# Where side steps stand between matmuls: other rates for two lanes, and three longer waits in steps

## The chip, the cores and the metric

The kernel runs on one core of a Trainium2 chip. The metric is the device time of one execution in microseconds (us). Runs of this kernel are compared by their medians. The engines are called as the profile calls them: PE is the matrix engine (PEld its weight loads), DVE the vector engine, ACT the scalar engine, POOL the general engine, and SP the engine that here issues nearly all DMAs, in the order in which they stand in its queue.

## The reference, cut to what matters

One layer of a hybrid encoder works on two request groups, which share their weights: `x_sample` (1024 rows) and `x_prompt` (256 rows), each of width 2048.

```
hn   = rms_norm(x);  proj = hn @ w_in
xbc, z_ssd, dt_raw, q, k, v, z_att, mq, z_mem = split_cols(proj)
y    = ssd_scan(forward) + ssd_scan(backward) + d_skip * xs      # chunks of 128, 16 heads, running sums of dt * A
o_ssd = rms_norm(y * silu(z_ssd))
o_att = window_attention(norm(q), norm(k), v, sink) * silu(z_att) # |t - s| <= 128, 8 heads, 2 key heads
mk, mv = split_cols(rms_norm(mem) @ w_mem_kv)
o_mem = softmax(norm(mq) @ norm(mk)^T) @ mv * silu(z_mem)         # 4 heads, 256 memory rows
out   = x + concat[o_ssd, o_att, o_mem] @ w_out
```

Everything is float32. A product with a weight matrix is made of three reduced-precision products, from a high and a low part of each factor.

## The kernel before

**Tiles and blocks.** The 1280 rows are 10 tiles of 128: tiles 0 to 7 are `x_sample`, 8 and 9 `x_prompt`. The big products run over groups of five tiles, group 0 (tiles 0 to 4) and group 1 (tiles 5 to 9). The program is a row of blocks: the memory keys and values, part of group 0 in `block_pair` units (a seven-product scheme), the blocks `kv` and `z1` of group 0, then group 1 (`x0` to `x5`, `kv`, `q`, `za`, `z0`, `z1`, `mq`, `zm`), then the output blocks `o` and the output in pairs. A block loops over 16 slices `k` of the width. For each slice SP loads a weight tile `wraw` (four buffers), ACT makes its high part `wh` (L206), DVE the low part `wl` (L207, three buffers each), and PE makes the products (L258 to L260, or L293 to L295) into PSUM tiles `acc`.

**Lanes.** All other work (key preparation, attention, memory attention, the scan) is cut into steps by `yield` and stands in two queues, the lanes. Lane 0 holds `vectors`, `distances`, `mk_prep`, `k_prep`, `attn`, `mem_attn`; lane 1 holds `dt_prep`, `ssd_up`, `ssd_down`. After each slice `pump` runs steps: the table `RATES` gives, for each group and block, how many steps of lane 0 and of lane 1 a slice pays for (half as many per slice in the blocks that `feat` runs, which are `x`, `za` and `zm`).

```
owed[i] = owed[i] + rates[i] if lanes[i] else 0.0
while max(owed) >= 1: ...
    step(lanes[i])
```

So a `yield` is a place where products of the block are put between what a step has issued and what the next step issues. A bare `yield` more makes the distance longer by one step of that lane, and puts every later step of the lane back by one. `need(fn, ts)` runs the lanes until the named work is done, whatever the rates say. The instructions then go through a scheduler that may move them a little within their engine's order; the order on an engine is fixed when the kernel is built.

**The three places of the change.** `mk_prep` (L428) prepares one 128-row tile of the memory keys: SP loads it (`mkr` from `mr`, L430), ACT squares it (L436), DVE sums (L437), POOL takes a power (L123, L124), DVE scales twice (L442, L443), and after two bare yields PE turns the four heads (`pmk`, L448). `dt_prep` (L518) computes the steps `dt` of five tiles in a long chain of small DVE operations, has POOL make a triangular mask, and after one bare yield PE forms the running sums (`pacs`, L557 to L559). `ssd_down` (L1012) first issues the loads for one tile of the backward scan, among them the turned diagonal product (`ydT` from `yd`, L1035), and after three bare yields (five for the first tile of a request, `last`) `norm_ssd` scales the tile before, and `diag_in` has PE turn the loaded tile (`pd`, L1041), which DVE adds.

Of the kernel before, what the change touches and what calls it, by code (L numbers as in the profile page):

```python
# [28 lines left out]
CH, WB, RB, WA, WBB = 4, 3, 4, 5, 4  # L29
RBB = 4  # L30

RATES = ({'kv': (2.0, 1.0), 'z1': (3.0, 1.6)},
         {'kv': (1.4, 1.5), 'x': (2.1, 2.15), 'q': (2.2, 2.5), 'za': (2.05, 2.5), 'z0': (2.0, 2.6),
          'z1': (1.9, 2.65), 'mq': (1.9, 2.8), 'zm': (1.9, 2.85), 'o': (1.95, 2.1)})
FAR = 1e30

UNITS = (0, 8, 1, 9, 2, 10, 3, 11, 4, 12, 5, 13, 6, 7)
# [7 lines left out]
def hymba_encoder_kernel(  # L45
# [37 lines left out]
    def psum(name):  # L83
        return mix.tile([P, 512], F32, tag="mix", name=name)
# [37 lines left out]
    def rsqrt(dst, src, scale, n):  # L122
        G.tensor_scalar(out=dst, in0=src, scalar1=scale, scalar2=EPS, op0=ALU.mult, op1=ALU.add)  # L123
        G.tensor_tensor(out=dst, in0=dst, in1=mhalf[:, :n], op=ALU.pow)  # L124

    def hv(ap, n=8):
        return ap.rearrange("p (h d) -> p h d", h=n)

    def hb(ap, n, d):
        return ap.unsqueeze(2).broadcast_to([P, n, d])  # L130
# [90 lines left out]
    def w_in_rows(name):  # L221
        return w_laid(laid_in(name), W_AT[name][1])
# [107 lines left out]
    def ev_dtkv(base):  # L330
        def f(i, ps):
            t = base + i
            r = ev.tile([P, P], F32, tag="evt" if i % 2 else "evu", name="kraw")
            A.activation(r, ps[:, 32:160], AF.Copy)
            S.dma_start(k_d[t], r)
            V.tensor_add(dt_all[:, t, :], ps[:, :32], dtb)
            V.tensor_copy(v_all[:, i + (2 if base else 0), :], ps[:, 160:288])
        return f
# [76 lines left out]
    def w2(name):  # L415
        return mp.tile([P, 512], F32, tag="wa", name=name, bufs=WA)
# [11 lines left out]
    def mk_prep(i):  # L428
        kr = w2("mkr")
        S.dma_start(kr, mr_d[i])  # L430
        yield
        yield
        ss = sm.tile([P, 4], F32, tag="s4", name="ss", bufs=4)
        sq = w2("sq")
        rm = rx[:, 10 + i:11 + i]
        A.activation(sq, kr, AF.Square, scale=rm)  # L436
        V.reduce_sum(out=ss, in_=hv(sq, 4), axis=AX.X)  # L437
        r = sm.tile([P, 4], F32, tag="s4", name="r", bufs=4)
        rsqrt(r, ss, 1.0 / P, 4)
        yield  # L440
        yield
        V.scalar_tensor_tensor(out=hv(kr, 4), in0=hv(kr, 4), scalar=rm, in1=hb(r, 4, P), op0=ALU.mult, op1=ALU.mult)  # L442
        V.tensor_mul(hv(kr, 4), hv(kr, 4), gm.unsqueeze(1).broadcast_to([P, 4, P]))  # L443
        yield
        yield
        ps = psum("pmk")
        for h in range(4):
            T.transpose(ps[:, h * P:(h + 1) * P], kr[:, h * P:(h + 1) * P], ident)  # L448
        c = slice((i % 2) * P, (i % 2) * P + P)
        if i < 2:  # L450
            A.activation(mkH[:, :, c], hv(ps, 4), AF.Copy)
            V.tensor_sub(mkL[:, :, c], hv(ps, 4), mkH[:, :, c].bitcast(F32))
        else:
            o = w2("mko")
            A.activation(o, ps, AF.Copy)
            S.dma_start(mk_d[:, :, c], hv(o, 4))
        yield
# [60 lines left out]
    def dt_prep(t0):  # L518
        grp = t0 // 5
        ts = slice(t0, t0 + 5)  # L520
        flat = lambda a: a[:, ts, :].rearrange("p t h -> p (t h)")
        t6 = (t0 + 1) % 6
        wj, dd = [a[:, t6:t6 + 5, :].rearrange("p t h -> p (t h)") for a in (wj_all, dd_all)]
        t5 = lambda a: a.rearrange("p (t h) -> p t h", t=5)
        x = flat(dt_all)
        e, s = [mp.tile([P, 512], F32, tag="xs", name=n, bufs=2)[:, :160] for n in "es"]
        w, l = [mp.tile([P, 512], F32, tag="ya", name=n, bufs=2)[:, :160] for n in "wl"]
        V.scalar_tensor_tensor(out=e, in0=x, scalar=-1.0, in1=x, op0=ALU.mult, op1=ALU.min)
        A.activation(e, e, AF.Exp)
        V.tensor_scalar(out=s, in0=e, scalar1=2.0, scalar2=None, op0=ALU.add)  # L530
        V.reciprocal(out=s, in_=s)
        V.tensor_mul(s, s, e)
        V.tensor_mul(w, s, s)
        V.tensor_scalar(out=e, in0=w, scalar1=1.0 / 17, scalar2=None, op0=ALU.mult)
        for c in (15, 13, 11, 9, 7, 5, 3):
            V.scalar_tensor_tensor(out=e, in0=e, scalar=1.0 / c, in1=w, op0=ALU.add, op1=ALU.mult)
        V.scalar_tensor_tensor(out=e, in0=e, scalar=1.0, in1=s, op0=ALU.add, op1=ALU.mult)
        V.tensor_scalar(out=e, in0=e, scalar1=2.0, scalar2=None, op0=ALU.mult)
        V.scalar_tensor_tensor(out=x, in0=x, scalar=0.0, in1=e, op0=ALU.max, op1=ALU.add)
        yield  # L540

        da = e
        V.tensor_mul(t5(da), dt_all[:, ts, :], aneg.unsqueeze(1).broadcast_to([P, 5, 32]))
        yield

        V.tensor_scalar(out=w, in0=x, scalar1=1e-30, scalar2=None, op0=ALU.max)
        V.tensor_scalar(out=l, in0=w.bitcast(I32), scalar1=math.log(2.0) / 2 ** 23, scalar2=-126.957 * math.log(2.0),
                        op0=ALU.mult, op1=ALU.add)
        yield
        yield  # L550
        lower = w2("lower")[:, :P]
        G.affine_select(out=lower, in_=ones, compare_op=ALU.is_ge, fill=0.0, base=0,
                        pattern=[[-1, P]], channel_multiplier=1)
        yield
        ps = psum("pacs")
        p5 = t5(ps[:, :160])
        T.matmul(p5[:, :, 0:16], upper, t5(da)[:, :, 0:16], start=True, stop=True)  # L557
        T.matmul(p5[:, :, 16:32], lower, t5(da)[:, :, 16:32], start=True, stop=True)
        T.matmul(ps[:, 160:320], ones, da, start=True, stop=True)  # L559
        ac = wb("ac", shape=(P, 512))  # L560
        A.activation(ac[:, :320], ps[:, :320], AF.Copy)
        for _ in range(2):
            A.activation(s, l, AF.Exp)
            d = da
            V.tensor_sub(d, w, s)
            V.tensor_add(s, w, s)
            V.reciprocal(out=s, in_=s)
            V.tensor_mul(d, d, s)
            V.scalar_tensor_tensor(out=l, in0=d, scalar=2.0, in1=l, op0=ALU.mult, op1=ALU.add)
        A.activation(flat(eacs_all), ac[:, 0:160], AF.Exp)  # L570
        A.activation(flat(cd_all), ac[:, 160:320], AF.Exp)
        V.tensor_sub(wj, l, ac[:, 0:160])
        V.tensor_add(dd, wj, ac[:, 160:320])
        A.activation(dd, dd, AF.Exp)
        yield
        ps = psum("pact")
        T.transpose(ps[:, :P], ac[:, 0:128], ident)
        T.transpose(ps[:32, P:2 * P], ac[:, 128:160], ident)
        acT = wb("acT", shape=(P, 512))
        A.activation(acT[:, :P], ps[:, :P], AF.Copy)  # L580
        A.activation(acT[:32, P:2 * P], ps[:32, P:2 * P], AF.Copy)
        S.dma_start(ac_d[grp][0:P, :], acT[:, :P])
        S.dma_start(ac_d[grp][P:160, :], acT[:32, P:2 * P])
        yield
# [216 lines left out]
    def wb(name, dtype=F32, shape=(P, 512)):  # L801
        return mp.tile(list(shape), dtype, tag="wb", name=name, bufs=WBB)
# [207 lines left out]
    def ssd_down(t):  # L1010
        first = t in (0, NS)
        last = t in (NS - 1, NT - 1)  # L1012
# [28 lines left out]
                T.transpose(ps[:, j * P:(j + 1) * P].bitcast(F32R), ld[g][3][:, j, :], identr)  # L1041
            V.tensor_add(ld[g][0], ld[g][0], ps)

        for _ in range(5 if last else 3):
            yield
        norm_ssd()
        diag_in(0)
# [1 line left out]
        for g in range(2):  # L1049
            c = slice(g * 512, (g + 1) * 512)  # L1050
            y, z, st, _ = ld[g]
# [461 lines left out]
    def tok(name, w, evac, after=None, grp=0):  # L1513
        run(block_tok(w, 5, evac), RATES[grp][name], after)

    def feat(name, b, evac, grp, after=None, extra=None):
        run(block_feat(f"{name}{b}", evac), [r / 2 for r in RATES[grp][name]], after, lag=3, extra=extra)

# [7 lines left out]
    for u, unit in enumerate(units):  # L1526
# [42 lines left out]
    w_kv = w_in_rows("kv")  # L1569
    run(block_tok(w_kv, 5, ev_dtkv(0), before_last=lambda _: need(vectors, [0])), RATES[0]["kv"], hold=5,  # L1570
        extra=lambda k: some_left() if left else None)
# [4 lines left out]
    def when_done(n, then):  # L1576
# [11 lines left out]
    queue(0, mem_attn, range(5))  # L1588
    run(block_tok(w_in_rows("z1"), 5, ev_gate(1, 0)), RATES[0]["z1"], refill_x(1),
        extra=when_done(1, lambda: queue(1, ssd_up, range(4))))  # L1590
# [12 lines left out]
    kv_shift()  # L1603
    run(block_tok(w_kv, 5, ev_dtkv(5)), RATES[1]["kv"], extra=lambda k: some_left() if left else None)
    queue(0, k_prep, range(5, 10))
    queue(0, attn, [4])
    queue(1, dt_prep, [5])
    run(block_tok(w_in_rows("q"), 5, ev_raw(q_d, 5)), RATES[1]["q"], extra=when_done(2, lambda: queue(1, ssd_up, range(4, 8))))
    gate("za", 0)
# [108 lines left out]
```

## Time and profile before

| | |
|---|---|
| median of 3 runs | 1802.68 us (1802.52 to 1804.86) |
| the profiled execution's own time | 1801.42 us |
| span of the profile | 1799.7 us |
| PE busy | 1779.4 us, 10838 matmuls |
| DVE, ACT, POOL busy | 1249.6, 920.7, 545.1 us |
| granted PE clock | 1.0 |
| moved by DMA | 301.12 MB, mean 167 GB/s |

PE is busy in all but about 20 us of the span, so the time is what PE has to do, and what it waits for. The list of waits names each wait by who ended it, with the total, the number of times and the longest; windows give busy times by stage; the timeline shows single instructions. Where an engine's wait ended on something that the profile cannot name, it says "issue". Matmuls overlap, so the times of single ones add up to more than the time that PE is busy; from start to start is what one costs.

### The profile page before, as it was taken

To read this page: it belongs to the slowest core of one execution; us is meant where nothing else is said; L and a number is where in the kernel's file an instruction comes from. 1 tells how busy PE (TensorE), PEld (TensorE's weight loads), DVE (VectorE), ACT (ScalarE), POOL (GpSimd) and SP (SyncE) were. 2 spreads that over 40 slices of the span, in tenths; PEclk is the share of its full clock that TensorE was granted. 3 is DMA by queue.
4 is the path that set the end of the run, shared out by engine and by line. 5 is a ranking of instruction groups with operands and counts; after the bars stand their busy time and mean duration, and the time that the engine had idled before them with its cause. 6 is when DMAs were issued, how large, how long until landed. Compare 5 with 4: busy or idle time off the path is not lost.

```text
span 1799.7 us, 31431 instructions
## 1 busy us (share of the span) xinstructions
PE 1779.4 (99%) x10838; PEld 1605.1 (89%) x10838; DVE 1249.6 (69%) x2358; ACT 920.7 (51%) x2049; POOL 545.1 (30%) x900
## 2 busy tenths in 40 slices
PE   9999999999999999999999999999999999999999
PEld 7789999999997989999889977777878888889999
DVE  5595788888758887877675566567774644766665
ACT  6554455555325765757464466534374533443332
POOL 0105789989710210000000000001100000058775
PEclk9999999999999999999999999999999999999999
DMA  8653455444446645444645545558685765644442
GB/s 296 192 179 120 139 152 151 136 150 152 125 146 201 193 136 167 121 141 121 183 143 163 177 152 168 192 162 256 218 253 169 235 186 151 205 149 147 143 145 77
DMA packets 208207, 301.12 MB, mean 167 GB/s; under 512 B 19568, under 2 KB 86192, under 8 KB 208048
## 3 DMA queue, kind: packets, MB, share of 16 engines
q1 hardware_dynamic: 207904, 299.06, 53.9%
q8 instruction: 85, 1.39, 0.3%
q14 instruction: 74, 0.61, 0.1%
q10 hardware_dynamic: 144, 0.06, 0.0%
HBM read 236.36 MB, written 62.69 MB: 166 GB/s over the span
## 4 chain that ended last, share of the span: by engine, by line
PE 82%; issue 5%; DMA 5%; DVE 4%; ACT 3%; POOL 1%; SPq 0%; ACTq 0%; DVEq 0%; POOLq 0%
PE acc L258 9%; PE acc L259 9%; PE acc L260 9%; PE acc L1231 7%; PE acc L1233 7%; PE acc L1232 7%; PE acc L293 4%; PE acc L295 4%; PE acc L294 4%; PE accm L1232 3%; PE accm L1231 3%; PE accm L1233 3%; PE po L671 1%; PE pmo L780 1%; PE ppt L661 1%
## 5 line engine op out<-in xcount | busy, mean ns | idle before, releaser
L207 DVE TENSOR_TENSOR wl<-wraw,wh 128x512 fp32r<-128x512 f32 (+1 forms) x480 | 346.0, 723 | 236.4 <-ACT wh L206 223.5
L206 ACT ACTIVATE wh<-wraw 128x512 fp32r<-128x512 f32 (+1 forms) x480 | 292.2, 614 | 311.1 <-PE acc L260 155.9
L258 PE MATMUL acc<-wh,xH 128*128 128x512 f32 (+1 forms) x1088 | 418.7, 385 | 0.0
L259 PE MATMUL acc<-wl,xH 128*128 128x512 f32 (+1 forms) x1088 | 413.0, 380 | 0.9 <-DVE wl L207 0.8
L260 PE MATMUL acc<-wh,xL 128*128 128x512 f32 (+1 forms) x1088 | 409.9, 377 | 0.0
L259 PEld LDWEIGHTS acc<-wl,xH 128*128 128x128 f32 x1088 | 204.8, 188 | 40.5 <-issue 3.6
L260 PEld LDWEIGHTS acc<-wh,xL 128*128 128x128 f32 x1088 | 204.3, 188 | 38.1 <-issue 1.7
L258 PEld LDWEIGHTS acc<-wh,xH 128*128 128x128 f32 x1088 | 204.6, 188 | 37.4 <-issue 3.3
L293 PE MATMUL acc<-xH,wh 128*128 128x320 f32 x640 | 201.7, 315 | 0.0
L206 ACT ACTIVATE sh<-ws 128x384 fp32r<-128x384 f32 x176 | 91.3, 523 | 212.5 <-POOL ws L1203 107.5
L294 PE MATMUL acc<-xL,wh 128*128 128x320 f32 x640 | 199.2, 311 | 0.0
L295 PE MATMUL acc<-xH,wl 128*128 128x320 f32 x640 | 198.6, 310 | 0.0
L207 DVE TENSOR_TENSOR sl<-ws,sh 128x384 fp32r<-128x384 f32 x176 | 124.2, 709 | 100.7 <-ACT sh L206 96.7
L1203 POOL TENSOR_TENSOR ws<-wraw 128x128 f32<-128x128 f32 x176 | 109.4, 622 | 213.2 <-DMA wraw<-in_w_in_pairs_dram 87.1
L633 POOL COPY lg<-nsink 128x2 f32<-128x2 f32 x40 | 17.1, 428 | 386.9 <-PE ppt L661 139.4
L293 PEld LDWEIGHTS acc<-xH,wh 128*128 128x128 f32 x640 | 120.2, 188 | 2.6 <-issue 2.0
L294 PEld LDWEIGHTS acc<-xL,wh 128*128 128x128 f32 x640 | 120.3, 188 | 1.5 <-issue 1.2
L295 PEld LDWEIGHTS acc<-xH,wl 128*128 128x128 f32 x640 | 120.2, 188 | 1.2 <-issue 1.1
L1203 POOL TENSOR_TENSOR ws<-wraw,ws 128x128 f32<-128x128 f32 x176 | 116.6, 663 | 13.8
L1203 POOL TENSOR_TENSOR ws<-ws,wraw 128x128 f32<-128x128 f32 x176 | 116.1, 660 | 0.0
L1203 POOL TENSOR_TENSOR wraw<-wraw 128x128 f32<-128x128 f32 x176 | 111.2, 632 | 13.7
L362 DVE SCALAR_TENSOR_TENSOR c<-u,vec,c 128x638 f32<-128x638 f32 (+1 forms) x96 | 89.6, 936 | 15.2 <-ACT c L357 14.9
(437 smaller groups left out, 3941.9 us busy)
## 6 DMA issues: line engine op xcount, KB each, us to landing
wraw<-in_w_in_laid_dram SPq DMA_DIRECT2D x176, 256.0 KB, 3.0
wraw<-in_w_in_pairs_dram SPq DMA_DIRECT2D x112, 256.0 KB, 2.8
wraw<-in_w_out_laid_dram SPq DMA_DIRECT2D x64, 256.0 KB, 3.0
wraw<-in_w_out_pairs_dram SPq DMA_DIRECT2D x64, 256.0 KB, 2.7
rf<-ac SPq DMA_DIRECT2D x40, 256.0 KB, 3.8
rb<-ac SPq DMA_DIRECT2D x40, 256.0 KB, 4.9
wraw<-in_w_mem_laid_dram SPq DMA_DIRECT2D x32, 256.0 KB, 4.6
xst<-in_x_sample_dram SPq DMA_DIRECT2D x20, 256.0 KB, 5.0
```

What stands on the lines that cost most here:

```text
L206: a = A.activation(h, raw, AF.Copy)
L207: b = V.tensor_sub(l, raw, h.bitcast(F32))
L258: T.matmul(ps[t][:, :n], sh, h[:, :n], start=(k_ == 0), stop=False)
L259: T.matmul(ps[t][:, :n], sh, l[:, :n], start=False, stop=False)
L260: T.matmul(ps[t][:, :n], sl, h[:, :n], start=False, stop=(k_ == KT - 1))
L293: T.matmul(o, sh, cur["H", q][:, m, c], start=(k == 0), stop=False)
L294: T.matmul(o, sh, cur["L", q][:, m, c], start=False, stop=False)
L295: T.matmul(o, sl, cur["H", q][:, m, c], start=False, stop=(k == KT - 1))
L1203: G.tensor_tensor(out=o, in0=x, in1=y, op=op)
L1231: T.matmul(ps[p], h, xh, start=(k_ == 0), stop=False)
L1232: T.matmul(ps[p], h, xl, start=False, stop=False)
L1233: T.matmul(ps[p], l, xh, start=False, stop=(k_ == 7))
```

## The change

The table of rates gets other numbers for four blocks, and three places get further bare yields. In group 0's `kv` block lane 0 goes from 2.0 to 4.0 steps a slice; in `z1` after it from 3.0 to 2.2, and lane 1 from 1.6 to 1.7. In group 1, lane 0 goes from 1.9 to 1.6 in `zm`; in the output blocks `o` from 1.95 to 2.15 and lane 1 from 2.1 to 2.25. `mk_prep` waits three steps instead of two before its transposes, `dt_prep` two instead of one before its running sums, and `ssd_down` nine instead of five before its first diagonal product, in the first tile of a request only. No instruction is added to or taken from the computation.

```
-RATES = ({'kv': (2.0, 1.0), 'z1': (3.0, 1.6)},
+RATES = ({'kv': (4.0, 1.0), 'z1': (2.2, 1.7)},
          {'kv': (1.4, 1.5), 'x': (2.1, 2.15), 'q': (2.2, 2.5), 'za': (2.05, 2.5), 'z0': (2.0, 2.6),
-          'z1': (1.9, 2.65), 'mq': (1.9, 2.8), 'zm': (1.9, 2.85), 'o': (1.95, 2.1)})
+          'z1': (1.9, 2.65), 'mq': (1.9, 2.8), 'zm': (1.6, 2.85), 'o': (2.15, 2.25)})
...
         V.tensor_mul(hv(kr, 4), hv(kr, 4), gm.unsqueeze(1).broadcast_to([P, 4, P]))
+        yield
         yield
         yield
         ps = psum("pmk")
...
                         pattern=[[-1, P]], channel_multiplier=1)
+        yield
         yield
         ps = psum("pacs")
...
-        for _ in range(5 if last else 3):
+        for _ in range(9 if last else 3):
             yield
         norm_ssd()
         diag_in(0)
```

In the orders below, line numbers of the changed kernel are higher by one behind the first new line and by two behind the second.

**SP, around the load of the fourth tile of memory keys (`mr_198`), in group 0's `z1` block.** `wraw` is a weight tile, `rf` and `rb` are rows of running sums spread over all partitions, `chd` a slice of the turned input. Before:

```order
L213 DMA wraw<-in_w_in_laid_dram 128x512
L848 DMA rf<-ac_193 128x512
L188 DMA chd<-in_x_turned_dram 128x640 x2
L848 DMA rb<-ac_193 128x512
L213 DMA wraw<-in_w_in_laid_dram 128x512
L848 DMA rf<-ac_193 128x512
L848 DMA rb<-ac_193 128x512
L213 DMA wraw<-in_w_in_laid_dram 128x512
L848 DMA rb<-ac_193 128x512 x2
L430 DMA mkr<-mr_198 128x512
```

And in the changed kernel:

```order
L335 DMA k_146<-kraw 128x128
L335 DMA k_147<-kraw 128x128
L335 DMA k_148<-kraw 128x128
L213 DMA wraw<-in_w_in_laid_dram 128x512 x3
L430 DMA mkr<-mr_198 128x512
L457 DMA mk_d<-mko 512x1x128
L213 DMA wraw<-in_w_in_laid_dram 128x512 x2
L188 DMA chd<-in_x_turned_dram 128x640
```

The load has moved from behind the spread rows and the input slices to ahead of them; the PE order puts the transposes that need it 90 products behind the start of `z1`, where they stood at 157.

**DVE, at the end of group 0's `kv` block.** `wl` of 128x288 is the low part of one of this block's 16 weight tiles, the first of 128x512 belongs to `z1`; `ss`, `mkr` and `mkL` are `mk_prep`'s, `dist` and `pdist` are `distances`'. Before, the last four tiles of the block:

```order
L207 TENSOR_TENSOR wl<-wraw,wh 128x288 x2
L1462 CAST dist<-disti 128x384
L1463 SCALAR_TENSOR_TENSOR dist<-dist 128x384
L207 TENSOR_TENSOR wl<-wraw,wh 128x288 x2
L1470 CAST pdist<-dist 128x384
L207 TENSOR_TENSOR wl<-wraw,wh 128x512
L437 TENSOR_REDUCE ss<-sq 128x4
L336 TENSOR_TENSOR dt_all<-acc,dtb 128x32
```

In the changed kernel, the last three:

```order
L207 TENSOR_TENSOR wl<-wraw,wh 128x288
L437 TENSOR_REDUCE ss<-sq 128x4
L442 SCALAR_TENSOR_TENSOR mkr<-mkr,rx,r 128x512
L207 TENSOR_TENSOR wl<-wraw,wh 128x288
L443 TENSOR_TENSOR mkr<-mkr,state 128x512
L207 TENSOR_TENSOR wl<-wraw,wh 128x288
L437 TENSOR_REDUCE ss<-sq 128x4
L453 TENSOR_TENSOR mkL<-pmk,mkH 128x4x128
L442 SCALAR_TENSOR_TENSOR mkr<-mkr,rx,r 128x512
L443 TENSOR_TENSOR mkr<-mkr,state 128x512
L207 TENSOR_TENSOR wl<-wraw,wh 128x512
L336 TENSOR_TENSOR dt_all<-acc,dtb 128x32
```

The DVE work of three tiles of memory keys now stands between the weight tiles of `kv`, ahead of the evacuation of the block's results (L336).

**SP, at the loads for tile 4 of the backward scan, at the end of group 1's `mq` block.** `yd_176` is that tile's diagonal product in DRAM, `so` a finished output tile on its way out, `zd` a gate, `st` a state. Before:

```order
L1033 DMA st_14576<-sb_186 128x512
L1033 DMA st_14584<-sb_186 128x512
L275 DMA wraw<-in_w_in_laid_dram 128x512
L1029 DMA zd<-z_4_112 128x512
L1008 DMA oT_1_161<-so 512x1x128
L698 DMA oT_1_155<-oT 512x1x128
L1035 DMA ydT<-yd_176 128x512
```

And in the changed kernel:

```order
L1028 DMA zd<-yT 128x4x128
L1019 DMA cc<-xbc_d 128x2x128
L1035 DMA st_14642<-sb_186 128x512
L1010 DMA oT_1_161<-so 512x1x128
L1037 DMA ydT<-yd_176 128x512
L1025 DMA yd<-yp_166 128x512
L1035 DMA st_14650<-sb_186 128x512
L1031 DMA zd<-z_4_112 128x512
```

The load of the diagonal product now stands ahead of the gate's load instead of behind it; on PE its use has moved from 187 to 210 products behind the start of `mq`.

More of the change, by code (lines that the diff above doesn't have):

```diff
@@ L30 @@
 RBB = 4
-RATES = ({'kv': (2.0, 1.0), 'z1': (3.0, 1.6)},
+RATES = ({'kv': (4.0, 1.0), 'z1': (2.2, 1.7)},
          {'kv': (1.4, 1.5), 'x': (2.1, 2.15), 'q': (2.2, 2.5), 'za': (2.05, 2.5), 'z0': (2.0, 2.6),
-          'z1': (1.9, 2.65), 'mq': (1.9, 2.8), 'zm': (1.9, 2.85), 'o': (1.95, 2.1)})
+          'z1': (1.9, 2.65), 'mq': (1.9, 2.8), 'zm': (1.6, 2.85), 'o': (2.15, 2.25)})
 FAR = 1e30
@@ L445, in mk_prep @@
         yield
+        yield
         ps = psum("pmk")
@@ L553, in dt_prep @@
                         pattern=[[-1, P]], channel_multiplier=1)
+        yield
         yield
@@ L1042, in diag_in @@
             V.tensor_add(ld[g][0], ld[g][0], ps)
-        for _ in range(5 if last else 3):
+        for _ in range(9 if last else 3):
             yield
```

## The prediction

> **What bounds the kernel now.** I read the page first, then the busy times by stage, then PE's list of waits, then the timeline around the longest of them. The page gives each engine's busy time, and of the chain that ended last the shares:
>
> ```profile
> PE 1779.4 (99%) x10838; PEld 1605.1 (89%) x10838; DVE 1249.6 (69%) x2358; ACT 920.7 (51%) x2049; POOL 545.1 (30%) x900
> PE 82%; issue 5%; DMA 5%; DVE 4%; ACT 3%; POOL 1%; SPq 0%; ACTq 0%; DVEq 0%; POOLq 0%
> ```
>
> PE is the bound. The change adds no instruction to it, so it can only act on the time in which PE stands. Busy times by stage (columns: stretch and length, PE, PEld, DVE, ACT, POOL with counts, clock, DMA share, GB/s) show where that is; the rows are group 0's `kv`, its `z1`, and `x` of group 1, then, with those between left out, `mq`, `zm` and `o`, and last a stretch of `o` without lane work:
>
> ```profile
> 496.00:529.00 33.00, 33.00 (x254) 33.00 (x253) 15.66 (x40) 9.11 (x23) 5.00 (x16) 1.00 0.53 159
> 529.00:594.00 65.00, 61.26 (x295) 50.42 (x293) 57.09 (x117) 34.12 (x77) 6.51 (x10) 1.00 0.62 195
> 594.00:821.00 227.00, 226.01 (x1594) 212.38 (x1593) 175.21 (x395) 141.67 (x351) 21.94 (x33) 1.00 0.46 142
> ...
> 1167.00:1246.00 79.00, 76.26 (x387) 58.57 (x385) 49.72 (x104) 31.64 (x76) 8.35 (x21) 1.00 0.64 200
> 1246.00:1335.00 89.00, 86.63 (x592) 77.65 (x590) 68.43 (x151) 47.95 (x117) 8.88 (x21) 1.00 0.76 234
> 1335.00:1598.00 263.00, 259.98 (x1309) 213.71 (x1308) 155.45 (x291) 122.62 (x267) 19.46 (x32) 1.00 0.61 187
> ...
> 1560.00:1590.00 30.00, 30.00 (x134) 24.86 (x133) 18.05 (x30) 13.10 (x23) 4.76 (x8) 1.00 0.40 114
> ```
>
> PE stands 3.7 us in `z1` of group 0, 1.0 in `x`, 2.7 in `mq`, 2.4 in `zm`, 3.0 in `o`: 12.8 us, which is all that the change could take back in these stages. The last row gives the price of a 512-wide product, 30/134 = 0.224 us, by which I turn products of an order into time. What ended PE's waits (total, times, longest):
>
> ```profile
> PE pd L1041 <- DMA ydT<-yd: 3.4, 2, 1.9
> PE pmk L448 <- issue: 3.1, 1, 3.1
> PE ppt L661 <- DVE oT L674: 1.5, 2, 0.9
> PE pst L863 <- ACT fh L877: 1.4, 1, 1.4
> ...
> PE po L671 <- ACT pT L662: 0.8, 1, 0.8
> PE pmt L765 <- DVE mpr L757: 0.8, 2, 0.6
> PE psc L639 <- DVE state L902: 0.8, 1, 0.8
> PE pr L1005 <- ACT pT L662: 0.6, 1, 0.6
> PE pacs L557 <- DVE w L546: 0.6, 1, 0.6
> ```
>
> The three transposes and sums that get further yields, `pd`, `pmk` and `pacs`, are 7.1 us of it.
>
> **Turned keys: -3.1 us.** "Issue" is resolved by the timeline (start, length):
>
> ```profile
> 559.51 0.32 SPq L430 DMA_DIRECT2D mkr<-mr  x1
> ...
> 565.97 0.72 ACT L436 ACTIVATE sq<-mkr,rx 128x512 f32<-128x512 f32 x1 [2.25 <-DMA mkr<-mr]
> 566.72 0.69 DVE L437 TENSOR_REDUCE ss<-sq 128x4 f32<-128x512 f32 x1 [1.83 <-ACT sq L436]
> ...
> 568.98 0.75 DVE L442 SCALAR_TENSOR_TENSOR mkr<-mkr,rx,r 128x512 f32<-128x512 f32 x1 [1.18 <-POOL r L124]
> ...
> 571.38 0.68 DVE L443 TENSOR_TENSOR mkr<-mkr,state 128x512 f32<-128x512 f32 x1
> ...
> 572.16 0.63 PE L448 MATMUL pmk<-identr,mkr 128*128 128x128 f32 x4 [3.14 <-issue]
> ```
>
> The fourth key tile's load took 6.4 us to land while the DMA engines were full, and square, sum, power and the two scalings followed in a row; PE waited for the last. The two rows of the DMA share there, and the spread of this load's landing over the four tiles:
>
> ```profile
> 560.00:564.00 4.00, 4.00 (x20) 3.28 (x19) 4.00 (x7) 3.20 (x6) 0.00 (x0) 1.00 1.06 365
> DMA to landing us min/median/max: 2.0/2.9/6.4
> ```
>
> In the changed order this load stands ahead of the spread rows and input slices, behind `z1`'s eighth weight tile. Four buffers of `wraw` and three of `wl` let that tile be issued when PE has done about one slice of `z1`, 529 + 15 x 0.224 = 532.4. Landed by 536 to 539, and with the 572.06 - 565.97 = 6.1 us of the chain above, the key tile is ready by 542 to 545; its transposes stand 90 products into the block, at 529 + 20.2 = 549.2. The wait goes, with 4 us in hand. Of the other three tiles' loads the first two move into `kv`; their price is below.
>
> **Running sums: -0.6 us.** `pacs` moves 15 products back (60 to 75 into `z1`), 3.4 us, against a wait of 0.6, and its chain has fewer key operations between. The step after it (`pact`) comes only 3 products later instead of 15, 0.7 us; ACT's copy between them takes 0.4, and the next operations of ACT are spread. I take nothing for it, 0 to 0.7.
>
> **Diagonal products: -1.9 us.** Both waits on `ydT` are not in a first tile, where nine yields now stand instead of five, but in tile 4 and tile 0. The SP queue's issue, PE's use, and the landing of all twenty:
>
> ```profile
> 1224.63 0.64 SPq L1035 DMA_DIRECT2D ydT<-yd  x1
> ...
> 1229.59 0.51 PE L1041 MATMUL pd<-identr,ydT 128*128 128x128 f32 x4 [1.85 <-DMA ydT<-yd]
> 1295.68 0.78 SPq L1035 DMA_DIRECT2D ydT<-yd  x1
> ...
> 1299.64 0.51 PE L1041 MATMUL pd<-identr,ydT 128*128 128x128 f32 x4 [1.50 <-DMA ydT<-yd]
> DMA to landing us min/median/max: 3.0/4.5/6.1
> SPq L1029 <- ACT zd L1065: 8.8, 5, 4.3
> ```
>
> Each load was issued 4 to 5 us ahead of its use and took about 4.5; SP came late to them because stores and gate loads stood ahead (the last row: SP's waits for a gate buffer, up to 4.3 us). What the four steps more do is to put all of lane 1 behind: every later tile of the scan meets other neighbours. For tile 4 the new order has the load ahead of the gate's load: -1.9. For tile 0, between the transposes whose store SP must issue first and the use there are 28 products of `zm` instead of 34; against that the queue ahead is shorter: I take 1.0 of the 1.5 as left, -0.5. Tile 3 loses room (its load now stands behind a store; 22 products between): +0.5. Ends: -3.4 (both go) and +1.0.
>
> A rule bears on this: the Trainium skill, "DMA: Bandwidth & Descriptors", section "Anatomy of one DMA", gives about 2.0 us fixed and the bytes at 436 GB/s, for 256 KB an estimate of 2.6 us. The rows disagree, 2.9 and 4.5 in the median; by the rule tile 3 would wait for nothing and the sum would be 0.5 us lower.
>
> **Four steps a slice in `kv`: +0.3 us.** This is the edit that has no cover shown, for the key work leaves `z1`, where DVE is busy 57.1 of 65 us, for the end of a block whose slices last 2 us. Prices there:
>
> ```profile
> 513.18 0.89 DVE L1433 COPY rbc<-prx 128x512 f32<-128x512 f32 x2
> 514.10 2.48 DVE L194 SCALAR_TENSOR_TENSOR chd<-chd,vec,rbc 128x640 f32<-128x640 f32 x3
> 518.15 0.45 DVE L207 TENSOR_TENSOR wl<-wraw,wh 128x288 fp32r<-128x288 f32 x1
> 526.53 0.69 DVE L437 TENSOR_REDUCE ss<-sq 128x4 f32<-128x512 f32 x1
> ...
> 527.58 1.04 POOL L124 TENSOR_TENSOR r<-r,mhalf 128x4 f32<-128x4 f32 x1
> ...
> 529.00 0.39 PE L258 MATMUL acc<-wh,xH 128*128 128x512 f32 x1
> ```
>
> From `pdist` (about 513.5) to `z1`'s first `wl` DVE now has: `rbc` 0.9, three sums 2.1, four slices of input 3.3, three and three scalings 2.2 + 2.0, one `mkL` 0.7, five `wl` 2.3, and 0.7: 14.2 us, less some 0.07 us of overlap in each of 20 (starts come closer than ends): 12.8. Twice it must also stand for POOL between sum and scaling (sum's end 527.22 to power's end 528.62, 1.4 us; once 0.7 of that is covered by `mkL`): 2.1. So 513.5 + 14.9 + 0.4 (pdist) = 528.8, and half a microsecond for the first evacuation: 529.3 against PE's 529.0. It just about fits. Ends: 0, and +3.5 where the first load takes 6.4 us to land instead of 2.9.
>
> **Side steps that now stand close: +0.7 us.** Lane 0 runs 45 to 70 products earlier from there to `zm`. So steps meet differently: the second query transpose and the scores behind it come within 0 to 6 products for attention tiles 0 to 3, where it was 23 to 48; against that the pairs behind the rows `psc` (0.8), `po` (0.8) and `pmo` have room again. Before, such pairs cost between nothing and 0.8 us each, so for eight new and seven gone I take +0.7, ends -2.5 and +5.
>
> **`zm` and `o`: +0.7 us.** The last scan tile of group 0 ends 24 products later (336 into `zm` instead of 312), so the loads of the output block's rows come later and their splits fall beside the steps that now wait 0.9 (`ppt`) and 1.4 (`pst`). Ends -2.3 (both go) and +3. The rates in `o` (2.15 and 2.25) bring lane ends 30 to 50 products forward, in a stretch where PE doesn't stand; nothing.
>
> **The sum.** -3.1 - 0.6 - 1.9 + 0.3 + 0.7 + 0.7 = -3.9 us. The profiled execution took 1801.42 us for a span of 1799.7, 1.26 less than the median of the runs, so it becomes 1797.5, and the median 1802.68 - 3.9 = 1798.8 us. The bound between "faster" and "the same" is 0.2% of the median, 3.6 us or 1799.1, about what a measurement of this kernel can tell from no change; the forecast lies just on the faster side.
>
> **The rivals.** *The waits only move.* Keys and sums gain 3.7, but `ydT` keeps its 3.4, since lane 1 is put back as a whole and not its loads ahead of its uses, and the close pairs cost 2: 1802.7 - 3.7 + 2 + 0.2 = 1801.2. For it: the two rows of `pd` are in tiles that got no yield. Against: the changed order of SP. Chance 0.28. *All waits of these kinds go*: -3.1 - 0.6 - 3.4 - 1.4 = -8.5, 1794.2; each step must fall well, chance 0.12. *Slower: key loads hold ACT in `kv`.* The squares stand in ACT's queue between `wh` splits; where the load is late, the splits behind it are late, and a slice of `kv` gives only 2 us of cover for each buffer. If the three loads take 6.4 us instead of 2.9, the chain grows by up to 3 x 3.5 = 10.5 us: -4.2 + 10.5 = +6.3, 1809.0. It makes the kernel slower than the bound from 7.8 us on, so all three must be late; the DMA share of 0.53 in `kv` speaks against it, the full engines three stages on (1.06) show that it happens. Chance 0.15. A wait of over 3.1 us would be longer than any in the trace, and by the row from 568 to 572 the clock stayed full:
>
> ```profile
> 568.00:572.00 4.00, 1.02 (x5) 0.51 (x3) 3.02 (x6) 0.00 (x0) 0.95 (x1) 1.00 0.60 215
> ```
>
> The Trainium skill, "TensorE: Matmul & The Clock Gate", Part 1, has the clock halve after an idle window of about 3.4 us, until as long a busy one: by it one longer wait in `kv` would cost about 1.7 us more (an estimate from that page); no run here shows such a wait. That the change does nothing is no case: the orders differ on every engine.
>
> **How the numbers follow.** The forecast case has 0.45 and a range of its own of 1796 to 1801.5; three quarters of it lie below 1799.1. Faster: 0.34 + 0.12 = 0.46. Same: 0.11 + 0.28 = 0.39. Slower: 0.15. The range reaches from the case where all waits go, 1794.2, to the start of the slower case, 1806.3: 1794 to 1806.5, with the slower case and little else left out.
>
> **What would show it.** `pmk` and `pacs` gone from PE's waits; `pd` at 1 to 2 us in place of 3.4; no stand of PE between 525 and 531. The prediction is wrong in its step on `kv` if PE stands over 1 us there, in that on lane 1 if `pd` waits over 3 us, and in that on close pairs if `psc`, `po`, `ppt` and `pmo` together wait over 5 us, against 3.5 now.

## The result, and the profile after

The changed kernel takes 1796.76 us in the median of 6 runs (1795.31 to 1799.73), the kernel before 1802.6 us (1800.84 to 1804.86). The ratio is 0.997, with a 95% interval of 0.9958 to 0.9983: 5.4 us faster, between 3.1 and 7.6. The forecast was 1798.8 us in a range of 1794.0 to 1806.5. The profiled execution took 1795.31 us for a span of 1793.6, 6.1 us less than the span before. Three executions of the experiments (2163 to 2318 us, at a granted clock of 0.70 to 0.75) are left out of the medians and ratios below.

The page's busy times say that PE has the same 10838 products and is busy 2.0 us less:

```profile
PE 1777.4 (99%) x10838; PEld 1606.1 (90%) x10838; DVE 1249.9 (70%) x2358; ACT 919.5 (51%) x2049; POOL 545.7 (30%) x900
```

PE's list of waits (total, times, longest) is an almost wholly new one, all of it here:

```profile
PE pcb L823 <- ACT pT L664: 2.7, 1, 2.7
PE pd L1043 <- DMA ydT<-yd: 2.7, 2, 2.4
PE pxs L858 <- DVE xs L860: 1.5, 1, 1.5
PE warm L1503 <- DVE zero L1501: 1.3, 1, 1.3
PE pxs L858 <- ACT kL L510: 1.2, 1, 1.2
PE pmt L767 <- ACT wh L206: 0.8, 1, 0.8
PE ppt L663 <- DVE nm L643: 0.5, 1, 0.5
PE acc L1235 <- DVE wl L207: 0.4, 1, 0.4
PE acc L258 <- DVE v_all L337: 0.4, 1, 0.4
PE pst L865 <- DVE ya L883: 0.2, 1, 0.2
PE acc L259 <- DVE wl L207: 0.2, 1, 0.2
PE acc L1233 <- DVE yt L410: 0.2, 1, 0.2
```

`pmk` and `pacs` are gone; so are `psc`, `po`, `pmo` and `pr`. `pd` has kept 2.7 of its 3.4 us. In their places stand `pcb` and two waits on `pxs`, the transposes of the scan's input, which waited for nothing before. The lists sum to 15.8 us before and 12.1 after: -3.7 of the 6.1.

The fourth key tile, in the timeline from its load to its last scaling, and the `pmk` transposes of all four tiles (shortest, median and longest in ns, first and last start):

```profile
535.91 0.38 SPq L430 DMA_DIRECT2D mkr<-mr  x1
538.72 0.72 ACT L436 ACTIVATE sq<-mkr,rx 128x512 f32<-128x512 f32 x1 [0.46 <-DMA mkr<-mr]
543.62 0.75 DVE L442 SCALAR_TENSOR_TENSOR mkr<-mkr,rx,r 128x512 f32<-128x512 f32 x1 [0.90 <-POOL r L124]
544.41 0.69 DVE L443 TENSOR_TENSOR mkr<-mkr,state 128x512 f32<-128x512 f32 x1
L449 PE MATMUL pmk<-identr,mkr x16: 270/272/273, 522.5 to 552.3; 128*128 128x128 f32 x16
```

The load goes out at 535.9 instead of 559.5 and is squared 2.8 us later instead of 6.5. The tile is ready at 545.1, its last transpose starts at 552.3. The four key loads landed in 4.0, 2.8, 2.9 and 2.8 us, where it was 2.9, 3.0, 3.6 and 6.4 before.

### The profile page after: what moved, and what is told of

Its sections match the earlier page's. It is cut to its first block, busy times and chain, and to the rows that moved or that the text cites. A ratio compares the mean times of both kernels' runs of the same rounds, so it can differ in the third digit from the quotient of the medians.

```text
span 1793.6 us, 31444 instructions
## 1 busy us (share of the span) xinstructions
PE 1777.4 (99%) x10838; PEld 1606.1 (90%) x10838; DVE 1249.9 (70%) x2358; ACT 919.5 (51%) x2049; POOL 545.7 (30%) x900
```

## The experiments

Each is compared with runs of the kernel before, taken together with it on the same chip, and its ratio is to these. A difference such as "-4.9 us" is the ratio's distance from 1, times 1802 us.

**The change in two halves.** Group 0's part is the rates of `kv` and `z1` and the yields ahead of `pmk` and `pacs`, group 1's the nine yields and the rates of `zm` and `o`; each is applied alone, with the diff lines of the change.

> Group 0's part of the change alone: the rates of kv and z1, the third yield ahead of the turned keys, the second ahead of the running sums. Theory A (each wait hangs on its own place, and the parts add up): pmk (3.1 us) and pacs (0.6) are gone, acc L258 waits 0.4 at the first evacuation, the new waits on pxs (1.2 and 1.5) and pmt (0.8) of the changed kernel appear, the old ones on psc, po and ppt of lane 0 (2.2) go; pd keeps about 3.4 us. Sum -3.7 +0.4 +1.3 = -2.0 us, between -3.7 and -1. Theory B (the early keys are the whole gain, by what they free in z1 and behind it): all of the 5.8 us, -5 to -6.5.

> Group 1's part alone: nine yields in the first backward tile, and the rates of zm and o. Theory A: pmk stays at 3.1 us and pacs at 0.6; pd goes from 3.4 to about 2.7, in tile 3 instead of tiles 4 and 0; ppt, pst and pr at the start of o (2.9) make room for one wait on pcb (2.7): -1 to -2 us, and together with the other half it makes the whole of -5.8 within 2 us. Theory B: 0, within 1 us.

Group 0's part: 1798.4 us, ratio 0.9992 (0.9981 to 1.0004), -1.4 us and not clear of nothing. Group 1's part: 1794.83 us, 0.9967 (0.9957 to 0.9978), -5.9 us, as much as the whole change. The halves add up to -7.3 against -5.4 for both, within the intervals. Theory A had the first half about right and the second too small; theory B is out. In the first half's list the wait of the keys is gone, and in its place stand these, beside 2.7 on `pd`:

```profile
PE pxs L858 <- DVE xs L860: 1.9, 1, 1.9
PE pxs L858 <- DVE oT L676: 1.7, 1, 1.7
PE pr L1007 <- DVE yd L1044: 1.7, 1, 1.7
PE pmt L767 <- ACT wh L206: 1.5, 1, 1.5
```

In the second half's, `pmk` keeps 2.9, and from `mq` to the end of `o` (1166 to 1600) PE waits 3.8 us, for these, where the kernel before waits 7.7:

```profile
PE ppt L661 <- ACT pT L662: 1.6, 1, 1.6
PE pd L1041 <- DMA ydT<-yd: 1.5, 1, 1.5
PE pd L1041 <- DVE y L1060: 0.4, 1, 0.4
PE pr L1005 <- DVE oT L674: 0.3, 1, 0.3
```

**Group 1's part in two.**

```
-        for _ in range(5 if last else 3):
+        for _ in range(9 if last else 3):
```

This alone in the first kernel, and in the second alone

```
-          'z1': (1.9, 2.65), 'mq': (1.9, 2.8), 'zm': (1.9, 2.85), 'o': (1.95, 2.1)})
+          'z1': (1.9, 2.65), 'mq': (1.9, 2.8), 'zm': (1.6, 2.85), 'o': (2.15, 2.25)})
```

> The nine yields alone. Theory A: pd loses its wait in tile 4 (1.9 us) and gets one in another tile, 1 to 2.7 us in all: between -2.4 and -0.7. Theory B (a put-back lane only moves its waits): pd 3 to 4 us, time within 1 us of before.

> The rates of zm and o alone. Theory A: pd in tile 4 keeps its 1.9 us (it lies in mq, ahead of these rates), the three waits at the start of o (2.9 us) change by -2.9 to +1, as lane 0 is put back by about a fifth in zm. Theory B: these rates alone give the 2.9 us.

The nine yields alone: 1799.98 us, 0.9995 (0.9986 to 1.0005), no change: `pd` waits 2.4, as theory A had it, but 2.1 on a `pcb` has come. The rates alone: 1804.61 us, 1.0023 (1.0013 to 1.0033), 4.1 us slower. Both together gave -5.9. So neither edit has a price of its own: each moves one lane, and the waits come from how the lanes then stand to each other. The rates alone, in PE's waits from 1166 to 1600:

```profile
PE pd L1041 <- DMA ydT<-yd: 2.9, 2, 1.7
PE pxs L856 <- ACT pT L662: 2.9, 1, 2.9
PE pmt L765 <- DVE mpr L757: 2.2, 1, 2.2
```

Against before, `pst`, `ppt` and `pr` (2.9 us) are gone, as both theories allowed, and a `pxs` at the first product of `o` (2.9) and a `pmt` further on (2.2) have come. That theory A forecast "-2.9 to +1" and got a slower kernel is a miss. The waits do not show the 4.1 us: they sum to 8.0 here and to 7.7 before. Most of it goes with PE's clock, which was granted at half for 3.4 us behind three of the waits in this kernel's trace (the last section has the rows). The mean clock of its twelve executions is 0.996 to 0.999, that of the kernel before beside them 0.998 to 1.000; at 0.998 two executions of the one took 1802.1 us in the mean, eleven of the other 1802.3.

**The other way round: the changed kernel with five yields again** (`range(9 if last else 3)` back to `range(5 if last else 3)`).

> The changed kernel with five yields in the first backward tile again. Theory A (nine yields and the rates of zm and o only gain together, since the rates alone cost 3.3 us and the yields alone gave 1.4): slower than the changed kernel by 4 to 8 us, about as slow as before or slower, and the waits in mq, zm and o come to 7 to 9 us instead of 5.5. Rival (group 0's part changes what the two do): within 2 us of the changed kernel.

1799.26 us, 0.9989 (0.9978 to 1.0001): 2.0 us below before, 3.4 above the changed kernel. The direction is theory A's, the size a little under its 4 to 8, and the two intervals overlap, so it is not clear of noise; a loss against the kernel before did not come. The waits in `mq`, `zm` and `o` are 7.3 us, inside its 7 to 9.

**The load of the diagonal product first.** In the changed kernel `pd` waits 2.4 us in tile 3, at 1250.74. The SP queue's issues ahead of it:

```profile
1237.81 3.06 SPq L327 DMA_DIRECT2D mq<-qs  x3
1242.58 0.33 SPq L409 DMA_DIRECT2D yt<-in_x_sample_dram  x1
1243.01 0.38 SPq L327 DMA_DIRECT2D mq<-qs  x1
...
1244.57 0.53 SPq L1010 DMA_DIRECT2D oT<-so  x1
1245.14 0.62 SPq L1037 DMA_DIRECT2D ydT<-yd  x1
```

The load stands behind the stores of the `mq` block's results (`mq` from `qs`), which SP can issue only as ACT evacuates them (three waits, 2.2 us), behind a load (`yt`, L409) that waits 1.7 us for such a store, and behind the store `oT`. Two kernels issue it first in its tile, ahead of the loads of `y` and the gate:

```
         for g in range(2):
...
+            d = mp.tile([P, 4, P], F32R, tag="rb", name="ydT", bufs=RBB)
+            S.dma_start(d.bitcast(F32), yd_d[t][:, 4 * g:4 * g + 4, :])
             y = mp.tile([P, 512], F32, tag="ya" if t % 2 else "rf", name="yd", bufs=2)
...
-            d = mp.tile([P, 4, P], F32R, tag="rb", name="ydT", bufs=RBB)
-            S.dma_start(d.bitcast(F32), yd_d[t][:, 4 * g:4 * g + 4, :])
```

> The changed kernel, with the load of the turned diagonal product issued first in each tile of the backward scan, ahead of the loads of y and of the gate, which wait for buffers. Theory A (pd waits because SP comes late to its load): both waits on pd go, 2.7 us, and if nothing takes their place the time is 2 to 3 us below the changed kernel's. Rival (the load is early enough already and the transfer itself is slow, or its own buffer is late): pd keeps 2 us or more, and SP, which now waits for that buffer ahead of all other loads of the tile, makes others late: the time is 0 to 3 us above the changed kernel's.

> Group 1's part of the change alone (nine yields, rates of zm and o), with that load issued first. Theory A: pd loses its 1.5 us against the same kernel without the earlier load, so 7 to 8 us below the kernel before. Rival: as fast as without it, 5 to 7 us below, or slower.

In the changed kernel it brings nothing: 1796.54 us, 0.997 (0.9959 to 0.9982), with `pd` still at 2.4. SP's queue there shows why (this kernel's SP issues):

```profile
1245.32 0.53 SPq L1010 DMA_DIRECT2D oT<-so  x1
1245.89 1.14 SPq L1025 DMA_DIRECT2D ydT<-yd  x2
```

The load still goes out behind the store, and 5.6 us ahead of its use, as without the edit; only what stood behind it has changed. With group 1's part alone, where lane 0 stands elsewhere, the same edit puts it ahead of the store:

```profile
1242.90 0.56 SPq L1023 DMA_DIRECT2D ydT<-yd  x1
1243.59 0.57 SPq L1008 DMA_DIRECT2D oT<-so  x1
```

PE uses it at 1247.41 without a wait, and the time is 1792.72 us, 0.9953 (0.9937 to 0.9968), 8.5 us below the kernel before; its interval overlaps that of group 1's part alone, so the time by itself does not prove the gain. Without the edit the load went out 3.4 us before PE was ready for it and landed in 4.7; with it, 4.5 us before and landed in 4.1. So the larger part of the wait came from SP's lateness, the rest from a slower landing; that an edit to the program's order reaches SP only if the lanes let it is shown by the other kernel.

**Which edit removes the wait of the keys.** The change's line for `kv` and `z1` alone, and its `yield` in `mk_prep` alone:

> The rates of kv and z1 alone. Theory A (the early load is what removes the wait of the turned keys; the third yield adds room that is not needed): pmk is gone, pacs waits 0 to 0.7, the new waits on pxs and pmt stand as with the whole of group 0's part. Time within 2 us of before. Rival (the third yield does it): pmk waits 1 to 2 us.

> The third yield ahead of the turned keys alone, at the old rates. Theory A: the transposes stand five products later for each key tile, so pmk in the fourth waits 2.0 us or less instead of 3.1, as the load's issue moves with the lane only where its own tile's steps do; time within 2 us of before. Rival (the load moves back by as much as its use): pmk keeps 3 us.

The rates alone: 1799.34 us, 0.9991 (0.998 to 1.0002). The wait in the fourth tile is gone, but the third tile's transposes now stand at the start of `z1` and wait 0.9 us for DVE's scaling; the third yield is what covers that, which theory A had as room not needed. New waits came elsewhere than forecast (`pk` 1.8 us, `pmt` in `o`). The third yield alone: 1799.79 us, 0.9987 (0.9976 to 0.9998), -2.3 us. It leaves 0.4 us of `pmk`, less than I said, since the load moved too (issued at 565.14) and fell into a time in which it landed in 5.2 instead of 6.4 us. A wait of 2.8 us on `pk` has come:

```profile
PE pk L506 <- ACT kh L498: 2.8, 1, 2.8
PE pmk L449 <- PE acc L260: 0.4, 1, 0.4
```

**The keys moved, and nothing else.** The question left was where the 3.7 us of `pmk` and `pacs` went, since group 0's part is worth only 1.4. This kernel moves the memory keys as the change does and then holds lane 0 back by 18 bare steps, at the old rates in `z1`. On PE nothing but the 16 key transposes changes its place: every other step of both lanes stands between the same products as before the change.

```
-RATES = ({'kv': (2.0, 1.0), 'z1': (3.0, 1.6)},
+RATES = ({'kv': (4.0, 1.0), 'z1': (3.0, 1.6)},
...
         V.tensor_mul(hv(kr, 4), hv(kr, 4), gm.unsqueeze(1).broadcast_to([P, 4, P]))
+        yield
         yield
         yield
...
     def k_prep(t):
+        yield from [None] * (18 if t == 0 else 0)
         r = w2("kr")[:, :P]
```

> The kernel before with the memory keys alone moved: four steps a slice in kv and the third yield, the old rates in z1, and 18 bare steps ahead of the first k_prep, by which every later step of both lanes stands on PE between the same products as before. Theory A (the wait of the turned keys is worth its length, and what gave it back was the meeting of later steps that lane 0's lead brought): pmk is gone, acc L258 waits 0.2 to 0.4, pacs keeps 0.6, pxs in z1 and x wait for nothing, psc and ppt of lane 0 wait as before; 2 to 3.5 us below the kernel before. Rival (the time comes back in z1 whatever the order, because DVE or the DMA engines are full there): within 1 us of before.

> The same move of the memory keys added to group 1's part with the diagonal product's load first. Theory A: its 2 to 3 us add to the 8.4 us (0.47%) that this part gave: 10 to 11.5 us below the kernel before, 4.5 to 6 us below the changed kernel. Rival: 7.5 to 9 us below before, as without it.

On the kernel before: 1796.69 us, 0.9973 (0.9964 to 0.9981), -4.9 us. PE's waits from 490 to 1165, `kv` to `z1` of group 1, come to 2.8 us instead of 5.8; `pmk` (3.1) is gone, and no `pxs` has come:

```profile
PE ppt L663 <- DVE oT L676: 0.9, 1, 0.9
PE pmo L782 <- ACT mpT L771: 0.6, 1, 0.6
PE acc L293 <- DVE zs L309: 0.4, 1, 0.4
PE po L673 <- ACT pT L664: 0.4, 1, 0.4
PE acc L258 <- DVE v_all L337: 0.3, 1, 0.3
PE pmt L767 <- DVE mpr L759: 0.2, 1, 0.2
```

So the whole of the keys' wait is to be had, and what gives it back in the changed kernel is not the early key work in `kv` and `z1` itself but what follows it: lane 0's lead above all. (Group 0's part also has lane 1's rate of 1.7 and the yield ahead of `pacs`, which no run took apart from the lead. `pacs`, which was to keep 0.6, does not wait either.) The 4.9 us are more than theory A's 3.5 and more than the wait. In executions with a mean clock of 1.000 the difference is 3.0 (1796.4 us in ten, 1799.4 in five of the kernel before): the wait's own length. The rest goes with the clock, for the kernel before reached 1.000 in only 5 of 22 executions and this one in 10 of 12. Added to group 1's part with the load first, it gives the fastest kernel of the study: 1789.61 us, 0.9939 (0.9924 to 0.9954), 11 us below the kernel before; its interval lies wholly below the changed kernel's. Its list from 1160 to 1600 holds two waits:

```profile
PE ppt L663 <- ACT pT L664: 1.2, 1, 1.2
PE pd L1043 <- DVE y L1062: 0.4, 1, 0.4
```

## Why the prediction was right, and where it was not

The forecast of a small gain held, and its total was 1.5 to 1.9 us short. Its parts did not hold equally.

**Turned keys (-3.1): right.** The load was forecast to go out at 532.4, land by 536 to 539, and the tile to be ready by 542 to 545. It was 535.9, 538.7 and 545.1; SP came 3.5 us later than I had it, and the landing was short. The transposes started 7 us after the tile was ready. (The 2.0/2.9/6.4 that the prediction took for the four loads counts the stores of these tiles too.)

**Running sums (-0.6): right.** `pacs` is gone, and `pact` does not wait.

**Four steps in `kv` (+0.3): right.** PE waits once, at the first product of `z1`:

```profile
530.00 0.47 PE L258 MATMUL acc<-wh,xH 128*128 128x512 f32 x1 [0.35 <-DVE v_all L337]
```

The slower rival had nothing to stand on: the key loads that moved into `kv` landed in 2.8 to 4.0 us.

**Diagonal products (-1.9): the step on tile 3 was mis-sized.** `pd` waits 2.7 us, where the prediction's sign of being right was 1 to 2. Tile 4's 1.9 us went, as forecast, and tile 0 kept 0.3 where I left it 1.0. But tile 3, to which I gave 0.5, waits 2.4; together -0.7. I saw the one store ahead of its load, and not that the tile had come to stand behind the end of the `mq` block, where SP waits for one evacuation after another. Its load was slow as well: PE could use it 5.6 us after its issue, where the twenty loads land in 4.6 in the median. The 2.6 us that the prediction takes from the Trainium skill ("DMA: Bandwidth & Descriptors", section "Anatomy of one DMA") is given there for the path of POOL's transfers, and SP issues these; none of the twenty landed in under 3.8.

**Side steps that stand close (+0.7): the step that failed.** I named the query transposes and the scores behind them as the new close pairs. They cost nothing, and the sign named for this step (`psc`, `po`, `ppt` and `pmo` together over 5 us) did not catch it: these four wait 0.5. From `z1` on, `psc`, `ppt`, `pmo` and a `pmt` of lane 0 lost 2.1 us of waits, and two on `pxs`, a `pmt`, a `ppt` and a `pst` came, 4.2 us together: +2.1. A `pxs` belongs to lane 1. One of the two (1.2) waits for work of lane 0, through a PSUM buffer (all these small products take theirs from one pool), as this piece of the timeline shows:

```profile
568.09 0.88 DVE L194 SCALAR_TENSOR_TENSOR chd<-chd,vec,rbc 128x640 f32<-128x640 f32 x1 [3.66 <-DMA chd<-in_x_turned_dram]
...
571.31 0.41 DVE L509 CAST kT<-pk 128x256 fp32r<-128x256 f32 x1
...
571.76 0.38 ACT L510 ACTIVATE kL<-pk 128x256 fp32r<-128x256 f32 x1 [4.79 <-DVE kT L509]
...
572.20 0.53 PE L858 MATMUL pxs<-identr,xc 128*128 128x128 f32 x4 [1.24 <-ACT kL L510]
```

DVE stood 3.66 us for an input slice in its queue; the cast of lane 0's keys stood behind it; ACT's copy waited for the cast; and PE's transposes for lane 1 waited for that copy. I had looked for pairs within one lane. The kernel with the 18 bare steps shows the size: without lane 0's lead the same move of the keys is worth 4.9 us instead of 1.4, and 3.0 instead of 0.5 in executions at a clock of 1.000.

**`zm` and `o` (+0.7): wrong sign, inside its ends.** From `mq` on, `po`, `ppt`, `pst`, `pr` and a `pmt` (4.3 us) went, and one wait of 2.7 on `pcb` came: -1.6, where the ends were -2.3 and +3. The mechanism of the new wait is the one named, splits of the output block's rows that fall late beside the steps:

```profile
1330.11 0.83 ACT L200 ACTIVATE xH<-chd,vec 128x640 fp32r<-128x640 f32 x1 [3.17 <-DMA chd<-oT]
...
1332.72 0.65 ACT L664 ACTIVATE pT<-ppt 128x256 f32<-128x256 f32 x2
...
1333.15 0.49 PE L823 MATMUL pcb<-bc 128*128 128x128 f32 x2 [2.73 <-ACT pT L664]
```

I priced the rates of `o` at nothing and the nine yields by `pd` alone. Tried one by one the two edits of this half give 0 and +4.1, together -5.9: a sum over edits could not have found that, since only the order that both make together has 3.8 us of waits there, where the yields alone have 6.7 and the rates alone 8.0.

**The sum by measured waits** is -3.1 - 0.6 - 0.7 + 0.4 + 2.1 - 1.6 = -3.5, against -3.9 forecast. That the total came out so near is partly luck: two terms that were too hopeful by 1.2 and 1.4 against one too dark by 2.3. The rest of the 5.4 us is not in the lengths of PE's waits. In the two profiled executions PE is busy 2.0 us less with the same products, at full clock in both up to the last microsecond; which of its instructions are shorter, or overlap more, no run here singled out. In the other executions a share can be the clock: the sum priced every wait at its length, and the prediction let the clock halve only behind a wait longer than any in the trace. The experiments show it halved behind waits of 1.7 to 3.0 us, at about 1.7 us each time, so a wait of that size can cost more than the sum gave it. How often it happened in this comparison's executions of the kernel before is not on record.

Of the rivals, "the waits only move" holds for group 0's half taken by itself (3.7 us gained, 2.1 given back), but not for the whole.

## What to carry to other kernels

In a kernel with a full engine and several queues of side work, an edit that removes a wait also moves everything behind it in its lane; price the two apart, and if the wait is worth having, hold the lane back afterwards so that the later steps meet as they did. Edits to two lanes that share PSUM buffers and one in-order queue per engine do not add up: try the pair before dropping either. Where a transpose waits for a buffer, look in the queues of the engines that empty it, the other lane's work among them, and where a load is late, at what the issuing queue waits for ahead of it, block ends above all. Compare executions at the same mean clock before a difference of a few us is put down to an edit: here a wait of 1.7 us or more could cost 1.7 us beyond its length.

## What the runs showed of the hardware

**Behind a wait PE's clock can run at half.** In nine of the eleven experiments' traces the granted clock reads 0.50 for stretches of 3.4 us (6.8 in one, group 1's part), each beginning within 1.6 us of the end of a wait of PE. Rows of the rates alone (columns as in the prediction), behind waits of 2.9 (`pmk`), 1.7 (`pd`) and 2.9 us (`pxs`):

```profile
571.00:573.00 2.00, 2.00 (x7) 1.63 (x6) 2.00 (x5) 1.37 (x3) 0.00 (x0) 0.50 0.36 128
1301.00:1304.00 3.00, 3.00 (x12) 2.43 (x10) 1.50 (x3) 0.78 (x2) 0.00 (x0) 0.50 0.41 131
1335.00:1338.00 3.00, 3.00 (x14) 2.51 (x14) 2.35 (x10) 2.15 (x9) 0.00 (x0) 0.50 1.02 279
```

In all thirteen traces together PE waits 1.6 us or longer 27 times. Behind 13 of these waits the clock halves, behind 14 it does not, among them the 3.1 us of `pmk` in the kernel before; behind shorter ones it never does. So length alone does not decide it, and what does stays open. Half the clock for 3.4 us is worth about 1.7 us (an estimate from these rows), and the executions agree: beside the kernel with the 18 bare steps the kernel before took 1799.4 us in the mean of five at a mean clock of 1.000, 1801.6 in eight at 0.999 and 1803.5 in seven at 0.998. All six executions of the fastest kernel, whose trace has no wait over 1.3 us, are at 1.000. They took 1790.2 us in the mean, 9.2 less than the kernel before at 1.000; its waits are 8.9 us shorter.

**A load's landing depends on when it is issued.** The same 256 KB load of the fourth key tile took 6.4 us to land where it was issued at 559.5 (before), 5.2 at 565.1 (third yield alone), and 2.8 at 535.9 (changed kernel), 24 us earlier in the same block. Where the load was moved to counted for as much as the room it gained: 3.6 us on the landing, against 3.4 more between issue and use.
